# Stick-breaking and forgetting layers: q and k projected with both activation halves in one 512-column matmul

## The chip, the cores and the metric

One core of one Trainium2 chip runs the whole program. The metric is the device time of one execution in microseconds (us); a median of several executions is compared. TensorE (PE) runs the matmuls, its weight loads are a stream of their own (PEld), VectorE (DVE) and ScalarE (ACT) do elementwise work and read the matmul accumulators in PSUM, GpSimd (POOL) does a little elementwise work on SBUF and issues some transfers, SyncE (SP) issues the weight loads.

## The reference

Four transformer layers run in sequence on 256 tokens of width 1024, all in fp32: a differential-attention layer and a MoBA layer (each with memory attention and a squared-ReLU MLP), then a stick-breaking layer and a forgetting layer, each followed by a gated convolution FFN. The change touches the projections of q and k in the last two:

```python
# stick-breaking
a = rmsnorm(h, sb_pre_g[layer])
q, k, v = jnp.split(a @ sb_w_qkv[layer], 3, axis=-1)     # 1024 -> 3 * 1024
o = stick_breaking_attention(split_heads(q), split_heads(k), split_heads(v))   # 16 heads of 64, q scaled by 0.125
...
# forgetting
s_in = rmsnorm(h, kv_norm_g)
kvf = s_in @ w_kvf                                       # k, v and the forget gates
a = rmsnorm(h, fox_pre_g[j])
q = split_heads(a @ fox_w_q[j])
o = forgetting_attention(q, k_sh, v_sh, fcum_sh)
```

## The kernel before

**Precision.** Every fp32 weight and activation of a projection is held as two fp32r tiles, a rounded value and the rest: for weights `whi` and `wlo` (made in `split`, L162 to L190, by one ACT copy and one DVE subtraction from the loaded `raw`), for activations the two halves of `yT`. A product is three matmuls (`mm3`, L211): hi by hi, hi by lo, lo by hi. `yT_tiles` (L247) lays the two activation halves of one 128-row chunk side by side, so that `y[:, k]` is 512 contiguous columns, 256 of the high half and then 256 of the low half.

**q and k of the last two layers.** The layers want q and k with the head dimension on the partitions, so a projection block gives 128 output columns (two heads) by 256 tokens. `layer_sb.qk(pr)` (L825) loads weights for two such blocks of q and two of k (`weights`, L192, in two pieces of four 128-row chunks), and is called for pr = 0, 2, 4, 6; `layer_fox.qk(g)` (L900) does the same for g = 0 to 3 with a gain on the weights, q and k from two matrices. In each, for i in 0 and 1, one accumulator tile of 512 columns takes two blocks, each by `columns_T` (L310): eight chunks of three 256-column matmuls, 24 in all. That makes 16 blocks in each layer, 32 in the program. The accumulators come from `acc_tile` (L83): two buffers of one PSUM bank.

**What reads the accumulators.** In the stick-breaking layer DVE multiplies each half by `R` (the row scales along the tokens, L315) into `qT` and `kT` (L833, L834). In the forgetting layer DVE does it per head, 64 partitions at a time, into `aug` (L915, L916). `quad` and `at` then make scores (`scores`, L354), weights and outputs.

**The up-projections.** `up_pair` (L511) already works in another way: per block eight matmuls of 512 columns with `whi` against both activation halves (L520), then eight of 256 columns with `wlo` against the high half (L522). The result stands in two halves of the bank, which ACT copies (L524) and DVE adds (L525).

**Order.** The text of the kernel is not the order of the engines' queues. A scheduler orders each engine's instructions from the dependences, and only a few places fix an order (`tc.issue_after`). The blocks of qk(4) and qk(6), and of the later g, are interleaved on PE with scores, transposes and outputs of the heads projected before them. Scratch tiles of 512 columns come from `t512`, a ring of five.

Of the kernel before, what the change touches and what calls it, by code (L numbers as in the profile page):

```python
# [10 lines left out]
AF = mybir.ActivationFunctionType  # L11
ALU = mybir.AluOpType
PSUM = bass.MemoryType.PSUM

S, D, P = 256, 1024, 128
NT = S // P
KC = D // P
# [40 lines left out]
def body(ctx, tc, d, out):  # L58
    nc = tc.nc
    mm = nc.tensor.matmul  # L60
    act = nc.scalar.activation
    V = nc.vector
# [11 lines left out]
    def t512(name):  # L74
        return ap_.tile([P, 512], F32, name=name, tag="ev", bufs=E_BUFS)
# [7 lines left out]
    def acc_tile(i=0):  # L83

        tag = ("acc", "pt", "po")[i]
        return pp.tile([P, 512], F32, name="acc", tag=tag, bufs=1 if i else 2)
# [4 lines left out]
    def sc_tile():  # L91
        return pp.tile([P, 512], F32, name="sc", tag="sc", bufs=2)
# [118 lines left out]
    def mm3(acc, a, b, start, stop):  # L211

        mm(acc, lhsT=a[0], rhs=b[0], start=start, stop=False)  # L213
        mm(acc, lhsT=a[0], rhs=b[1], start=False, stop=False)  # L214
        mm(acc, lhsT=a[1], rhs=b[0], start=False, stop=stop)  # L215
# [94 lines left out]
    def columns_T(acc, yT, ws, o):  # L310

        for k in range(KC):
            mm3(acc, tuple(h[:, o:o + P] for h in ws[k]), (yT[0][:, k, :], yT[1][:, k, :]), k == 0, k == KC - 1)
# [194 lines left out]
        V.tensor_tensor(lo, u, hi.bitcast(F32), op=ALU.subtract)  # L508
        return hi, lo

    def up_pair(yT, ws, o, j):  # L511

        s = t512("s")
        for i in range(2):
            b = sc_tile() if j == 0 else pp.tile([P, 512], F32, name="up", tag="ht", bufs=2)
            cs = slice(o + i * P, o + (i + 1) * P)
            for k in range(KC):
                mm(b, lhsT=ws[k][0][:, cs], rhs=yT[2][:, k].rearrange("p a s -> p (a s)"), start=k == 0, stop=False)  # L520
            for k in range(KC):
                mm(b[:, :S], lhsT=ws[k][1][:, cs], rhs=yT[0][:, k], start=False, stop=k == KC - 1)  # L522
            si = s[:, i * S:(i + 1) * S]
            act(si, b[:, S:], AF.Copy)  # L524
            V.tensor_tensor(si, b[:, :S], si, op=ALU.add)  # L525
        return s

    def up_tokens(yT, ws, f):
# [110 lines left out]
    ws = weights(kv_segs("a"), lambda: load_rows(mem, d["mem"], 1))  # L639
# [6 lines left out]
    ws = weights(kv_segs("b"))  # L646
# [173 lines left out]
    def layer_sb(yT, rs, first):  # L820
        w = d["sb_w_qkv_2"][0]
        qT, kT, v = qk_tiles()
        oT = yT_tiles()

        def qk(pr):  # L825

            ws = weights([(w, pr * P, 256, None), (w, D + pr * P, 256, None)])
            for i in range(2):
                acc = acc_tile()
                for j in range(2):  # L830
                    columns_T(acc[:, j * S:(j + 1) * S], yT, ws, (2 * j + i) * P)
                dst = (pr + i) // 4, (pr + i) % 4
                V.scalar_tensor_tensor(qT[dst[0]][:, dst[1]], acc[:, :S], 0.125, R, op0=ALU.mult, op1=ALU.mult)  # L833
                V.tensor_tensor(kT[dst[0]][:, dst[1]], acc[:, S:], R, op=ALU.mult)  # L834

        def vv(c):
            return ([(w, 2 * D + c * 512, 512, None)],
                    lambda t, acc: copy_to(v[:, t, c * 512:(c + 1) * 512], acc, rs[t]))

        def at(pr, t, n=2):  # L840
            quad(qT, kT, lambda b, h: v[:, b, h * 64:(h + 1) * 64], pr, t, True, oT, pr, stick, n)

        projs(yT, [vv(0), vv(1)], after=first)
        R = along_rows(rs)
        qk(0)
        qk(2)
        at(0, 0, 4)
        at(0, 1)
        qk(4)
        at(2, 1)  # L850
        qk(6)
        at(4, 0, 4)
        at(4, 1)
        at(6, 1)
        return OutProj(oT, d["sb_w_o_2"][0], list(range(KC)))


    def layer_fox(yT, rs, first):
        wkv, wq = d["w_kvf_2"], d["fox_w_q_2"][0]
        gk, gq = gain["kv_norm_g_2"], gain["fox_pre_g_2"]  # L860
        v = ap_.tile([P, NT, D], F32, name="vt", tag="vt", bufs=1)
        oT = yT_tiles()
        sums = tc.dram_tile([H2, 3, S], F32, name="sums")
        lf = cst.tile([P, NT, H2], F32, name="lf")
        bf = cst.tile([P, H2], F32, name="bf")
        with tc.issue_after(pows[3].ins):
            nc.gpsimd.dma_start(bf, bc_row(d["b_f_2"], H2))
        with tc.issue_after(last_gelu[0].ins):
            nc.scalar.preload_act_table_set("natural_log_exp_and_others")
        tri = con[:, C_TRI:C_TRI + P]  # L870
        one = con[:, C_ONE:C_ONE + P]
        lu = cst.tile([P, NT, H2], F32, name="lu")

        def v_f(t, acc):

            copy_to(v[:, t, D - 320:], acc[:, :320], rs[t])
            V.scalar_tensor_tensor(lu[:, t], acc[:, 320:], rs[t], bf, op0=ALU.mult, op1=ALU.add)
            if t == 0:
                return
            a = sm.tile([P, NT, H2], F32, name="fa", bufs=1)  # L880
            act(a, lu, AF.Abs)
            act(a, a, AF.Exp, scale=-1.0)
            act(a, a, AF.Ln, bias=1.0)
            V.scalar_tensor_tensor(lf, lu, 0.0, a, op0=ALU.min, op1=ALU.subtract)
            f = tp_tile()
            mm(f[:H2, 0], lhsT=lf[:, 0], rhs=tri, start=True, stop=True)
            mm(f[:H2, 1], lhsT=lf[:, 0], rhs=one, start=True, stop=False)
            mm(f[:H2, 1], lhsT=lf[:, 1], rhs=tri, start=False, stop=True)
            fr = ap_.tile([P, 4, S], F32, name="fr", tag="gb", bufs=1)
            act(fr[:H2, 0], f[:H2, :2], AF.Copy)  # L890
            act(fr[:H2, 2], f[:H2, :2], AF.Copy, scale=-1.0)
            V.memset(fr[:H2, 1], 1.0)
            nc.gpsimd.dma_start(sums, fr[:H2, :3])

        def vv(c0, n):
            return [(wkv, D + c0, n, gk)], lambda t, acc: copy_to(v[:, t, c0:c0 + n], acc, rs[t])

        aug = {}

        def qk(g):  # L900

            for q in (True, False):
                tag = "q" if q else "k"
                aug[g, q] = ap_.tile([P, 4, S], F32, name="aug", tag=tag + str(g % 2), bufs=1)

                row = 0 if q else 1
                nc.gpsimd.dma_start(aug[g, q][64:66], sums[g * 4:(g + 1) * 4, row:row + 2].rearrange("h r s -> r h s"))
            ws = weights([(wkv, g * 256, 256, gk), (wq, g * 256, 256, gq)])
            for i in range(2):
                acc = acc_tile()  # L910
                for j in range(2):
                    columns_T(acc[:, j * S:(j + 1) * S], yT, ws, (2 * j + i) * P)
                for c in range(2):
                    r = slice(c * 64, (c + 1) * 64)
                    V.tensor_tensor(aug[g, False][:64, 2 * i + c], acc[r, :S], R[r], op=ALU.mult)  # L915
                    V.scalar_tensor_tensor(aug[g, True][:64, 2 * i + c], acc[r, S:], 0.125, R[r],  # L916
                                           op0=ALU.mult, op1=ALU.mult)

        def at(g, t):
            nk = (t + 1) * P  # L920
            nb = t + 1
            o = tp_tile("ht")
            n = 2 if t else 4
            for h0 in range(0, 4, n):
                sv, = scores([[aug[g, True][:66, h0 + c] for c in range(n)]],
                             [[aug[g, False][:66, h0 + c] for c in range(n)]], t, nk)
                pT = weights_T(soft(sv, True, nk), nk)
                for j in range(0, n, 2):
                    for b in range(nb):
                        for c in range(2):  # L930
                            h = 4 * g + h0 + j + c
                            mm(o[c * 64:(c + 1) * 64, (h0 + j) // 2], lhsT=v[:, b, h * 64:(h + 1) * 64],
                               rhs=pT[:, (j + c) * nb + b], start=b == 0, stop=b == nb - 1)
            out_T(oT, t, o[:, :2], 2 * g)

        projs(yT, [([(wkv, 2 * D - 320, 320 + H2, gk)], v_f)])
        R = along_rows(rs)
        projs(yT, [vv(0, 384)])
        qk(0)
        qk(1)  # L940
        at(0, 0)
        at(0, 1)
        projs(yT, [vv(384, 320)])
        at(1, 0)
        qk(2)
        at(2, 0)
        at(1, 1)
        qk(3)
        at(3, 0)
        at(2, 1)  # L950
        at(3, 1)
        return OutProj(oT, d["fox_w_o_2"][0], list(range(KC)))
# [95 lines left out]
```

## Time and profile before

| | us |
|---|---|
| median of 3 runs | 1245.14 (1244.16 to 1249.25) |
| the profiled execution | 1245.2 |
| its span, first to last instruction | 1243.4 |
| PE busy in the span | 1222.5 |
| DVE busy | 905.6 |
| ACT busy | 753.9 |
| POOL busy | 44.8 |

The profiled execution is 0.06 us from the median; 1.8 us of it lie outside the span. PE's busy time counts overlapping matmuls once, and a matmul's recorded duration is longer than the distance to the start of the next one, so a pace is read from start to start. The granted TensorE clock is 0.998 of full speed over the span. The stick-breaking layer's q and k blocks run from 644.4 to about 705 us and the forgetting layer's from about 953 to 1016 us.

### The profile page before, as it was taken

To read this page: it belongs to the slowest core of one execution; us is meant where nothing else is said; L and a number is where in the kernel's file an instruction comes from. 1 tells how busy PE (TensorE), PEld (TensorE's weight loads), DVE (VectorE), ACT (ScalarE), POOL (GpSimd) and SP (SyncE) were. 2 spreads that over 40 slices of the span, in tenths; PEclk is the share of its full clock that TensorE was granted. 3 is DMA by queue.
4 is the path that set the end of the run, shared out by engine and by line. 5 is a ranking of instruction groups with operands and counts; after the bars stand their busy time and mean duration, and the time that the engine had idled before them with its cause. 6 is when DMAs were issued, how large, how long until landed. Compare 5 with 4: busy or idle time off the path is not lost.

```text
span 1243.4 us, 17840 instructions
## 1 busy us (share of the span) xinstructions
PE 1222.5 (98%) x6703; PEld 1022.0 (82%) x6703; DVE 905.6 (73%) x1677; ACT 753.9 (61%) x1363; POOL 44.8 (4%) x77
## 2 busy tenths in 40 slices
PE   8999999999999999999999999999999999999997
PEld 6876788888877788888889878888889997888886
DVE  5768756565776765756667888877788876987775
ACT  7665654454666654545555778666677755866663
POOL 1200100000000000000000010000001001000000
PEclk9999999999999999999999999999999999999999
DMA  9734356465452365655474416655537453565550
GB/s 322 220 135 140 123 179 220 152 207 200 154 185 102 103 203 179 215 181 183 156 232 158 135 58 206 207 181 197 203 111 244 143 158 115 193 205 180 179 193 34
DMA packets 125957, 214.21 MB, mean 172 GB/s; under 512 B 5280, under 2 KB 78304, under 8 KB 125872
## 3 DMA queue, kind: packets, MB, share of 16 engines
q1 hardware_dynamic: 123392, 207.25, 49.3%
q0 software_dynamic: 2336, 5.77, 1.7%
q8 instruction: 52, 0.85, 0.3%
q14 instruction: 33, 0.27, 0.1%
q10 hardware_dynamic: 144, 0.07, 0.0%
HBM read 211.96 MB, written 1.10 MB: 171 GB/s over the span
## 4 chain that ended last, share of the span: by engine, by line
PE 88%; DVE 4%; ACT 4%; issue 2%; DMA 1%; POOL 1%; SPq 0%; POOLq 0%; DVEq 0%; ACTq 0%
PE acc L213 12%; PE acc L215 12%; PE acc L214 12%; PE up L520 10%; PE sc L520 10%; PE up L522 5%; PE sc L522 5%; PE acc L292 4%; PE acc L293 4%; PE acc L295 4%; PE sc L360 2%; PE tp L399 2%; PE tp L449 2%; DVE wlo L175 2%; PE tp L257 1%
## 5 line engine op out<-in xcount | busy, mean ns | idle before, releaser
L175 DVE TENSOR_TENSOR wlo<-raw,whi 128x1024 fp32r<-128x1024 f32 x336 | 405.8, 1220 | 108.9 <-ACT whi L174 85.9
L174 ACT ACTIVATE whi<-raw 128x1024 fp32r<-128x1024 f32 x336 | 346.0, 1055 | 104.5 <-PE acc L215 60.2
L213 PE MATMUL acc<-whi,u 128*128 128x512 f32 x432 | 169.2, 392 | 0.0
L214 PE MATMUL acc<-wlo,u 128*128 128x512 f32 x432 | 168.6, 390 | 0.0
L215 PE MATMUL acc<-whi,u 128*128 128x512 f32 x432 | 168.0, 390 | 0.0
L520 PE MATMUL sc<-yT,whi 128*128 128x512 f32 x544 | 136.6, 391 | 0.0
L520 PE MATMUL up<-yT,whi 128*128 128x512 f32 x544 | 135.9, 392 | 0.0
L292 PE MATMUL acc<-whi,yT 128*128 128x512 f32 (+3 forms) x336 | 131.5, 394 | 0.0
L293 PE MATMUL acc<-wlo,yT 128*128 128x512 f32 (+3 forms) x336 | 130.0, 390 | 0.0
L520 PEld LDWEIGHTS sc<-yT,whi 128*128 128x128 f32 x544 | 99.7, 188 | 19.0
L520 PEld LDWEIGHTS up<-yT,whi 128*128 128x128 f32 x544 | 98.6, 189 | 18.1
L607 DVE SCALAR_TENSOR_TENSOR cv<-s,conv,cv 128x254 f32<-128x254 f32 (+1 forms) x160 | 76.1, 479 | 36.1 <-ACT cv L605 34.9
L215 PEld LDWEIGHTS acc<-whi,u 128*128 128x128 f32 x432 | 81.0, 188 | 17.9 <-DVE u L508 0.4
L213 PEld LDWEIGHTS acc<-whi,u 128*128 128x128 f32 x432 | 81.3, 188 | 16.3 <-ACT u L507 0.9
L214 PEld LDWEIGHTS acc<-wlo,u 128*128 128x128 f32 x432 | 81.3, 188 | 15.1
L295 PE MATMUL acc<-whi,yT 128*128 128x512 f32 (+3 forms) x336 | 84.5, 385 | 0.0
L185 DVE SCALAR_TENSOR_TENSOR wlo<-raw,g_late,whi 128x256 fp32r<-128x256 f32 (+4 forms) x128 | 68.2, 580 | 17.5 <-ACT whi L184 17.3
L522 PEld LDWEIGHTS up<-yT,wlo 128*128 128x128 f32 x544 | 74.2, 190 | 5.3
L522 PEld LDWEIGHTS sc<-yT,wlo 128*128 128x128 f32 x544 | 74.2, 190 | 5.2
L184 ACT ACTIVATE whi<-raw,g_late 128x256 fp32r<-128x256 f32 (+4 forms) x128 | 64.7, 577 | 20.4 <-PE acc L214 11.1
L522 PE MATMUL up<-yT,wlo 128*128 128x256 f32 x544 | 75.9, 282 | 0.0
L522 PE MATMUL sc<-yT,wlo 128*128 128x256 f32 x544 | 75.8, 282 | 0.0
(199 smaller groups left out, 1931.8 us busy)
## 6 DMA issues: line engine op xcount, KB each, us to landing
raw<-in_w_up SPq DMA_DIRECT2D x88, 512.0 KB, 4.5
raw<-in_w_down SPq DMA_DIRECT2D x22, 1024.0 KB, 5.0
raw<-in_a_w_up SPq DMA_DIRECT2D x16, 1024.0 KB, 5.3
raw<-in_a_w_down SPq DMA_DIRECT2D x16, 1024.0 KB, 5.0
raw<-in_b_w_up SPq DMA_DIRECT2D x16, 1024.0 KB, 5.3
raw<-in_b_w_down SPq DMA_DIRECT2D x16, 1024.0 KB, 5.0
raw<-in_sb_w_qkv SPq DMA_DIRECT2D x16, 512.0 KB, 5.0
raw<-in_a_w_in SPq DMA_DIRECT2D x6, 1024.0 KB, 7.5
```

The lines of the kernel that those rows point to most:

```text
L174: act(hv, rv[:, k0:k1], AF.Copy)
L175: V.tensor_tensor(lv, rv[:, k0:k1], hv.bitcast(F32), op=ALU.subtract)
L185: V.scalar_tensor_tensor(lv[:, k - k0, o:e], rv[:, k, o:e], gk, hv[:, k - k0, o:e].bitcast(F32), op0=ALU.mult, op1=ALU.subtract)
L213: mm(acc, lhsT=a[0], rhs=b[0], start=start, stop=False)
L214: mm(acc, lhsT=a[0], rhs=b[1], start=False, stop=False)
L215: mm(acc, lhsT=a[1], rhs=b[0], start=False, stop=stop)
L292: mm(acc, lhsT=h, rhs=ws[k][0], start=k == 0, stop=False)
L293: mm(acc, lhsT=h, rhs=ws[k][1], start=False, stop=False)
L295: mm(acc, lhsT=tslice(yT, k, t)[1], rhs=ws[k][0], start=False, stop=k == KC - 1)
L520: mm(b, lhsT=ws[k][0][:, cs], rhs=yT[2][:, k].rearrange("p a s -> p (a s)"), start=k == 0, stop=False)
L522: mm(b[:, :S], lhsT=ws[k][1][:, cs], rhs=yT[0][:, k], start=False, stop=k == KC - 1)
L607: V.scalar_tensor_tensor(hi[:, sh:], pi[:, :S - sh], cw(tap, ch), hi[:, sh:], op0=ALU.mult, op1=ALU.add)
```

## The change

`both_T` takes the matmul loops out of `up_pair`, and `added` the copy and the sum, with a scale. The q and k projections call these for each block, on an accumulator tile of its own, into a scratch tile `z` of 256 columns. In the stick-breaking layer GpSimd then multiplies `z` by `R` into `qT` or `kT`; in the forgetting layer DVE multiplies the two heads' 64 rows of `z` by `R` into `aug`. `up_pair` itself computes what it did.

```diff
+    def both_T(b, yT, ws, o):
+        cs = slice(o, o + P)
+        for k in range(KC):
+            mm(b, lhsT=ws[k][0][:, cs], rhs=yT[2][:, k].rearrange("p a s -> p (a s)"), start=k == 0, stop=False)
+        for k in range(KC):
+            mm(b[:, :S], lhsT=ws[k][1][:, cs], rhs=yT[0][:, k], start=False, stop=k == KC - 1)
+
+    def added(b, dst, scale=1.0):
+        act(dst, b[:, S:], AF.Copy, scale=scale)
+        V.scalar_tensor_tensor(dst, b[:, :S], scale, dst, op0=ALU.mult, op1=ALU.add)
...
     def up_pair(yT, ws, o, j):
...
-            si = s[:, i * S:(i + 1) * S]
-            act(si, b[:, S:], AF.Copy)
-            V.tensor_tensor(si, b[:, :S], si, op=ALU.add)
+            both_T(b, yT, ws, o + i * P)
+            added(b, s[:, i * S:(i + 1) * S])
...
             for i in range(2):          # layer_sb.qk
-                acc = acc_tile()
-                for j in range(2):
-                    columns_T(acc[:, j * S:(j + 1) * S], yT, ws, (2 * j + i) * P)
                 dst = (pr + i) // 4, (pr + i) % 4
-                V.scalar_tensor_tensor(qT[dst[0]][:, dst[1]], acc[:, :S], 0.125, R, op0=ALU.mult, op1=ALU.mult)
-                V.tensor_tensor(kT[dst[0]][:, dst[1]], acc[:, S:], R, op=ALU.mult)
+                for j, to in enumerate((qT, kT)):
+                    acc, z = acc_tile(), t512("cq")[:, :S]
+                    both_T(acc, yT, ws, (2 * j + i) * P)
+                    added(acc, z, 1.0 if j else 0.125)
+                    nc.gpsimd.tensor_tensor(to[dst[0]][:, dst[1]], z, R, op=ALU.mult)
...
             for i in range(2):          # layer_fox.qk
-                acc = acc_tile()
                 for j in range(2):
-                    columns_T(acc[:, j * S:(j + 1) * S], yT, ws, (2 * j + i) * P)
-                for c in range(2):
-                    r = slice(c * 64, (c + 1) * 64)
-                    V.tensor_tensor(aug[g, False][:64, 2 * i + c], acc[r, :S], R[r], op=ALU.mult)
-                    V.scalar_tensor_tensor(aug[g, True][:64, 2 * i + c], acc[r, S:], 0.125, R[r],
-                                           op0=ALU.mult, op1=ALU.mult)
+                    acc, z = acc_tile(), t512("cq")[:, :S]
+                    both_T(acc, yT, ws, (2 * j + i) * P)
+                    added(acc, z)
+                    for c in range(2):
+                        r = slice(c * 64, (c + 1) * 64)
+                        V.scalar_tensor_tensor(aug[g, j == 1][:64, 2 * i + c], z[r], 0.125 if j else 1.0, R[r],
+                                               op0=ALU.mult, op1=ALU.mult)
```

## Rows read from the trace of the kernel before

**Rows 1.** The page, busy us, share of the span and instructions of each engine:
```profile
PE 1222.5 (98%) x6703; PEld 1022.0 (82%) x6703; DVE 905.6 (73%) x1677; ACT 753.9 (61%) x1363; POOL 44.8 (4%) x77
```

**Rows 2.** The page, chain of work that ended last, share of the span by engine:
```profile
PE 88%; DVE 4%; ACT 4%; issue 2%; DMA 1%; POOL 1%; SPq 0%; POOLq 0%; DVEq 0%; ACTq 0%
```

**Rows 3.** Windows over both layers' q and k stretches:
```profile
core 0: us, PE busy (x) PEld busy (x) DVE busy (x) ACT busy (x) POOL busy (x), PEclk, DMA share, GB/s
644.00:668.00 24.00, 24.00 (x203) 23.74 (x203) 13.29 (x17) 10.16 (x12) 0.00 (x0) 1.00 0.73 244
668.00:692.00 24.00, 23.83 (x189) 20.26 (x186) 23.44 (x40) 18.05 (x30) 0.00 (x0) 1.00 0.35 118
692.00:716.00 24.00, 23.95 (x168) 19.46 (x166) 19.22 (x35) 16.34 (x26) 0.00 (x0) 1.00 0.45 146
...
953.00:987.00 34.00, 34.00 (x275) 32.52 (x274) 25.76 (x90) 20.86 (x58) 1.10 (x2) 1.00 0.57 186
987.00:1020.00 33.00, 32.91 (x263) 30.31 (x262) 25.93 (x74) 20.11 (x48) 1.66 (x3) 1.00 0.45 147
```

**Rows 4.** Timeline of PE, start us and duration, in qk(0), 75 matmuls apart:
```profile
644.88 0.28 PE L213 MATMUL acc<-yT,whi 128*128 128x256 f32 x1
...
653.88 0.28 PE L213 MATMUL acc<-yT,whi 128*128 128x256 f32 x1
```

**Rows 5.** Timeline of PE in the up-projection; the window cuts the last row:
```profile
773.20 1.98 PE L520 MATMUL sc<-yT,whi 128*128 128x512 f32 x8
775.02 1.11 PE L522 MATMUL sc<-yT,wlo 128*128 128x256 f32 x8
775.97 2.00 PE L520 MATMUL sc<-yT,whi 128*128 128x512 f32 x8
...
778.76 1.55 PE L520 MATMUL up<-yT,whi 128*128 128x512 f32 x6
```

**Rows 6.** Groups by line and form: busy us, mean ns, idle before and its releaser:
```profile
L213 PE MATMUL acc<-yT,whi 128*128 128x256 f32 x256 | 74.5, 291 | 0.0
...
L525 DVE TENSOR_TENSOR s<-sc,s 128x256 f32<-128x256 f32 x68 | 28.6, 421 | 38.6 <-ACT s L524 38.1
...
L524 ACT ACTIVATE s<-sc 128x256 f32<-128x256 f32 x68 | 26.0, 382 | 77.1 <-PE sc L522 76.8
...
L915 DVE TENSOR_TENSOR aug<-acc,R 64x256 f32<-64x256 f32 x16 | 6.7, 420 | 2.2 <-PE acc L215 2.0
L916 DVE SCALAR_TENSOR_TENSOR aug<-acc,R 64x256 f32<-64x256 f32 x16 | 6.6, 413 | 0.0
```

**Rows 7.** The same groups of DVE alone, 644 to 716 us:
```profile
L175 DVE TENSOR_TENSOR wlo<-raw,whi 128x1024 fp32r<-128x1024 f32 x20 | 24.0, 1219 | 10.2 <-ACT whi L174 9.9 <-PE tp L399 0.2
...
L436 DVE TENSOR_TENSOR ka<-ka,kb 128x512 f32<-128x512 f32 x7 | 4.8, 687 | 0.1
L833 DVE SCALAR_TENSOR_TENSOR qT<-acc,R 128x256 f32<-128x256 f32 x8 | 3.3, 416 | 2.1 <-PE acc L215 2.1
L834 DVE TENSOR_TENSOR kT<-acc,R 128x256 f32<-128x256 f32 x8 | 3.3, 411 | 0.0
```

**Rows 8.** Timeline of POOL, start us and duration, with idle before and releaser:
```profile
85.49 1.04 POOL L222 TENSOR_TENSOR rstd<-ms,mhalf 128x4 f32<-128x4 f32 x1 [46.96 <-DVE ms L229]
...
630.25 0.56 POOL L222 TENSOR_TENSOR rstd<-ms,mhalf 128x1 f32<-128x1 f32 x1 [1.96 <-DVE ms L240]
723.32 0.58 POOL L108 DMA_DIRECT2D gr<-in_ffn_pre_g  x1 [92.51 <-DVE ka L436]
```

**Rows 9.** Waits of PEld, 644 to 740 us: total, times, longest:
```profile
PEld sc L360 <- DVE kT L834: 0.9, 3, 0.4
```

**Rows 10.** Waits of PEld, 953 to 1040 us:
```profile
PEld sc L360 <- DVE aug L916: 0.5, 2, 0.2
```

**Rows 11.** Timeline of ACT, the weight splits of qk(4):
```profile
665.48 3.91 ACT L174 ACTIVATE whi<-raw 128x1024 fp32r<-128x1024 f32 x4 [7.62 <-PE acc L214]
```

**Rows 12.** Line L213, durations ns min/median/max:
```profile
L213 PE MATMUL acc<-yT,whi x256: 277/283/471, 644.4 to 1015.9; 128*128 128x256 f32 x128
```

More of the change, by code (lines that the diff above doesn't have):

```diff
@@ L517, in up_pair @@
             b = sc_tile() if j == 0 else pp.tile([P, 512], F32, name="up", tag="ht", bufs=2)
[L518 to L522, printed above, removed]
-            si = s[:, i * S:(i + 1) * S]
-            act(si, b[:, S:], AF.Copy)
-            V.tensor_tensor(si, b[:, :S], si, op=ALU.add)
+            both_T(b, yT, ws, o + i * P)
+            added(b, s[:, i * S:(i + 1) * S])
         return s
```

## Prediction

> **What bounds the kernel.** I read the page's busy times first, then its chain, then windows over the two stretches that change, and last the start-to-start pace of the matmuls. PE is busy for 98% of the span [rows 1] and carries 88% of the chain that ended last [rows 2]. In the windows the reader is to see that PE leaves almost nothing over in either stretch: 71.78 of 72 us from 644 to 716, 66.91 of 67 us from 953 to 1020, at full granted clock [rows 3]. The second thing to see is which engine stands next: DVE, with 23.44 of 24 us from 668 to 692, where attention runs between the projections, but only 13.29 of 24 before that [rows 3]. So a saving counts if it shortens PE's own stream, and a cost counts if it makes PE wait; work on ACT, DVE or POOL is free as long as it is not late for PE.
>
> **The matmuls.** A block of 128 output columns goes from 24 matmuls of 256 columns to eight of 512 and eight of 256. The columns streamed are the same, 6144. What differs is the number of matmuls. Before: 75 matmuls in 9.00 us from start to start, 0.120 us each, so 24 x 0.120 = 2.88 us a block [rows 4]. After: the up-projection is the new form exactly, and its blocks start at 773.20, 775.97 and 778.76, so 2.78 us a block in the mean [rows 5]. The difference is 0.10 us, and over 32 blocks 3.2 us. It is small because the long matmul costs nearly as much as two short ones: from 773.20 to 775.02 the eight long ones take 0.2275 us each, against 2 x 0.120 = 0.240 us [rows 4, 5]; what is fixed in a matmul is thus about 0.0125 us, and eight fewer of them are the 0.10 us. The bounds: nothing, if scores and transposes break up the new stream as often as the old, and 5.2 us, if also the excess over the typical matmul goes. That excess is read on L213: its mean is 291 ns and its median 283 ns, times 256 that is 2.0 us [rows 6, 12]. I take 3.2 us.
>
> The Trainium skill (TensorE: Matmul & The Clock Gate, "Wait — 56ns, not 53.3ns?") gives the fixed part of a warm matmul as about 2.5 ns, which would make the change worth 32 x 8 x 2.5 ns, some 0.6 us by estimate. The trace does not agree: its rows give 12.5 ns, five times that.
>
> **Order inside a block.** Before, the first three matmuls need `whi` and `wlo` of the first chunk; after, all `wlo` are needed only behind eight long matmuls, 1.8 us into the block. This can only help at a start. I count nothing for it, since no listed wait of these blocks is as long as that.
>
> **Evacuation.** Before, DVE reads the accumulator once per block in the stick-breaking layer (0.416 us for q, 0.411 us for k [rows 7]) and twice, by heads, in the forgetting layer (0.420 and 0.413 us [rows 6]). After, ACT copies a half (0.382 us) and DVE adds the other (0.421 us), as in the up-projection [rows 6]; then POOL (first layer) or two DVE operations (second) multiply by R.
> - ACT gains 32 x 0.382 = 12.2 us, half in each stretch. It is busy for 44.6 of 72 us and 41.0 of 67 us there [rows 3], so 6.1 us more is hidden by its idle time; without that cover it would cost those 6.1 us in each.
> - DVE in the stick-breaking layer exchanges one operation of 0.41 us for one of 0.42 us: nothing.
> - DVE in the forgetting layer gains one operation a block, 16 x 0.42 = 6.7 us, on 51.7 of 67 us [rows 3]. The 15.3 us idle hide it; without cover it would be all 6.7 us.
> - POOL gains 16 multiplies of 128x256. The trace has none. From below: the DVE multiply of this shape, 0.411 us [rows 7]. From above: POOL's power operation, whose duration rises from 0.56 us at one column to 1.04 us at four, 0.16 us a column [rows 8], which would make some 41 us. The nearest row in what is computed is DVE's, in the engine POOL's fixed part. I take 0.56 us plus 256 columns at DVE's pace between its 256 and 512 column forms, (687 - 411) / 256 = 1.1 ns [rows 7], together 0.84 us, and keep 41 us as the far bound. At 0.84 us a multiply takes a third of a block's 2.78 us and delays nobody on POOL.
>
> POOL's queue holds nothing else there: after the power operation at 630.25 its next entry is the transfer of `gr` at 723.32, which waits 92.51 us for a buffer that this very attention frees [rows 8]. The multiplies must stand ahead of it, or the attention would never end; the last of them falls near 707, so the transfer keeps its place. No other queue is moved: the weight loads on SP are the same.
>
> **Late arrivals at the scores.** The scores wait for the evacuated q and k. Before, the last block's chain is two DVE operations, 0.83 us. After, it is copy, add and multiply: 0.38 + 0.42 + 0.84 = 1.64 us in the first layer, and 0.38 + 0.42 + 2 x 0.42 = 1.64 us in the second. That is 0.8 us later. The waits that show it now are five, 0.9 us in three on `kT` and 0.5 us in two on `aug` [rows 9, 10]. If each grew by 0.8 us it would cost 4.0 us, if other blocks fill in, nothing. Blocks of later heads are at hand in most places; I take 0.3 of it, 1.2 us.
>
> **Sum.** On the profiled execution: 1245.2 - 3.2 + 1.2 = 1243.2 us, which is 1241.4 us of span and 1.8 us around it. The median of the runs is 1245.14, so nothing needs to be shifted. About 0.5% (6.2 us) is what a measurement can tell from no change, and this gain of 0.16% is below it.
>
> **Rivals.**
> - *PE waits for accumulators (slower).* There are two, and each now holds one block, not two, so a block must be evacuated within the 2.78 us of the next. Copy and add take 0.80 us, which leaves 1.98 us for both queues. One weight split ahead on each queue, 3.91 / 4 = 0.98 us on ACT and 1.22 us on DVE [rows 11, 7], is 2.20 us: a stall of 0.22 us at least; four splits in a row as at 665.48 would be 3.91 + 0.80 - 2.78 = 1.9 us. It decides from 0.3 us a block on: 32 x 0.3 = 9.6 us, less 3.2, and the time is 1251.6 us. For it: DVE's 23.44 of 24 us. Against it: from 668 to 705 PE spends 37 us on eight blocks with attention between, 4.6 us each, and before 668 both queues are half idle [rows 3]. Chance 0.16.
> - *POOL and DVE get in each other's way (no change).* If every multiply after 668, about ten, takes DVE's time as well, that is 8.4 us against the 5.3 us that DVE has idle from 668 to 716 [rows 3]: 3.1 us late, and 1246.3 us. No row here shows the two at work together. Chance 0.17. The Trainium skill (SBUF — State Buffer, "SBUF: two separate sides") has such a rule: an operation of DVE with two SBUF inputs and one of GpSimd that reads SBUF hold a shared port pair in turn, and one blocks the other for its whole length. The split and the sums of the stick-breaking weights have two SBUF inputs, so the rule would apply here; no row yet bears on it.
> - *The saving does not come (no change).* The interleaving eats the 3.2 us and the late arrivals remain: 1246.4 us. For it: the scheduler makes a new order from new durations. Against it: most of the blocks before 668 run without a break. Chance 0.05.
> - *Everything helps (faster).* 3.2 us, the 2.0 us of excess and the 1.4 us of waits on `kT` and `aug` all go: 6.6 us, 1238.6 us. Chance 0.09.
> - *The POOL multiply costs what the power operation suggests (slower).* From 2.78 us on POOL sets the pace; at 41 us, 16 of them are 656 us, largely exposed: some 1850 us. Chance 0.03, since a power is much more work per element than a product.
>
> **How the numbers follow.** The forecast has 0.50 and is 1243.2 us. Faster by over 0.5% (below 1238.9) is the fourth rival alone, 0.09; slower by over 0.5% (above 1251.4) the first and the fifth, 0.19; the rest, 0.72, is no change. The range goes from 1238.0, just beyond the case where all helps, to 1252.0, just beyond the first rival's point; the fifth rival and the longer stalls of the first lie outside it.
>
> **What would show it.** In the changed profile: 256 matmuls of 512 columns and 256 of 256 columns in place of 768, with a block's start-to-start at 2.78 us where nothing is between; PE's busy share in both stretches as before; the scores' waits longer by under 1 us. The first rival would show as waits of PE for ACT or DVE at the first matmul of a block; the second as split or `ka`, `kb` operations of DVE longer than 1.22 and 0.69 us while POOL works; the fifth as POOL busy in the stretch from 644 to 716. The prediction is wrong if the order on PE changes so that some stage runs out of work: a few us at the end of either layer would be enough, in either direction.

## The result and the profile after

The changed kernel takes 1254.57 us in the median of 8 runs (1247.98 to 1256.1), the kernel before 1245.34 us in 8 runs of its own beside it. The ratio is 1.0063 with an interval of 1.0052 to 1.0075: slower by 0.63%, and outside the predicted range. The eight runs fall into two groups. Six have a granted clock of 0.994 or 0.995 and take 1253.9 to 1256.1 us; two have 0.999 and take 1248.0 and 1248.2 us. So about 6.9 us go with the lower clock (medians of the groups 1255.0 and 1248.1 us), and some 2.7 us are lost without it.

The profiled execution took 1254.85 us. The page of the changed kernel, busy time by engine, beside [rows 1]:

```profile
PE 1226.4 (98%) x6447; PEld 1010.6 (81%) x6447; DVE 914.8 (73%) x1693; ACT 763.6 (61%) x1395; POOL 62.2 (5%) x93
```

Shares do not show the loss: PE is still 98% busy. ACT has gained 9.7 us, DVE 9.2 and POOL 17.4, and PE has the 256 matmuls fewer that the change makes. To find the place, I compare the same four events in both kernels, the `rstd` operation of POOL after each part. First the changed kernel, timeline of POOL:

```profile
631.59 0.56 POOL L222 TENSOR_TENSOR rstd<-ms,mhalf 128x1 f32<-128x1 f32 x1 [1.95 <-DVE ms L240]
...
757.76 0.56 POOL L222 TENSOR_TENSOR rstd<-ms,mhalf 128x1 f32<-128x1 f32 x1 [1.93 <-DVE ms L240]
...
946.97 0.55 POOL L222 TENSOR_TENSOR rstd<-ms,mhalf 128x1 f32<-128x1 f32 x1 [4.23 <-DVE ms L240]
...
1064.95 0.56 POOL L222 TENSOR_TENSOR rstd<-ms,mhalf 128x1 f32<-128x1 f32 x1 [1.92 <-DVE ms L240]
```

The kernel before, the same view (its first event is in [rows 8], at 630.25):

```profile
747.27 0.56 POOL L222 TENSOR_TENSOR rstd<-ms,mhalf 128x1 f32<-128x1 f32 x1 [1.93 <-DVE ms L240]
...
936.10 0.55 POOL L222 TENSOR_TENSOR rstd<-ms,mhalf 128x1 f32<-128x1 f32 x1 [4.22 <-DVE ms L240]
...
1055.31 0.56 POOL L222 TENSOR_TENSOR rstd<-ms,mhalf 128x1 f32<-128x1 f32 x1 [1.92 <-DVE ms L240]
```

The lag is 1.3 us before the stick-breaking layer, 10.5 us behind it, 10.9 us before the forgetting layer and 9.6 us behind it. So the stick-breaking layer loses 9.2 us, and the forgetting layer gains 1.2. Of the 1.3 us, 1.0 is there at the second `rstd` operation, at 14.15 us against 13.15, before anything that was changed; the up-projections of the earlier layers, whose sum on DVE now has a scale, add under 0.1 us.

Inside the losing layer, windows of the changed kernel (columns as in [rows 3]):

```profile
669.00:693.00 24.00, 22.39 (x104) 16.00 (x102) 18.44 (x32) 14.35 (x27) 4.90 (x4) 0.79 0.27 88
...
672.00:675.00 3.00, 2.82 (x12) 2.24 (x13) 2.29 (x3) 1.51 (x3) 0.13 (x1) 0.75 0.81 329
675.00:678.00 3.00, 3.00 (x10) 1.90 (x8) 2.64 (x7) 0.78 (x3) 0.00 (x0) 0.50 0.72 224
678.00:681.00 3.00, 3.00 (x7) 1.78 (x7) 1.82 (x5) 2.94 (x6) 1.10 (x1) 0.50 0.33 131
681.00:684.00 3.00, 3.00 (x12) 2.52 (x11) 3.00 (x8) 0.91 (x2) 0.00 (x0) 0.54 0.00 0
...
645.00:735.00 90.00, 85.61 (x474) 65.94 (x473) 66.05 (x101) 57.32 (x94) 16.82 (x16) 0.94 0.42 136
...
735.00:760.00 25.00, 22.90 (x129) 17.41 (x128) 20.43 (x37) 15.15 (x33) 3.94 (x7) 1.00 0.38 126
```

The same stretches of the kernel before, which reaches the end of the second one 10.5 us earlier:

```profile
645.00:735.00 90.00, 89.78 (x662) 76.29 (x661) 71.28 (x118) 58.24 (x92) 1.68 (x3) 1.00 0.42 137
735.00:749.50 14.50, 13.16 (x63) 10.23 (x62) 11.69 (x20) 8.28 (x19) 2.24 (x4) 1.00 0.51 181
```

Two things are to be seen. The granted clock falls to 0.50, TensorE's 1.2 GHz in place of 2.4: the shares of the first and the last of the four slices put this at about 673.5 to 683.8 us. The missing shares of the four slices are 0.75 + 1.5 + 1.5 + 1.4 = 5.1 us of PE's work. And PE is idle for 4.4 + 2.1 = 6.5 us over the two stretches, against 0.2 + 1.3 = 1.6 before: 4.9 us more. Less the saving in matmuls, 16 blocks by 0.09 (below), 1.4 us, this is 8.6 of the 9.2 us. The last 0.6 us I could not place, and the 5.1 us are less than the 6.9 us between the two groups of runs. Of the 4.9 us, 2.6 are waits of PE for `kT` (2.8 us against 0.2) and 2.5 are two later waits for ACT (`ka`, 1.6, and `pT`, 0.9) that PE does not have before; a shorter wait for `y` takes 0.2 off.

What PE does there, timeline of PE in the changed kernel:

```profile
645.77 2.07 PE L516 MATMUL acc<-yT,whi 128*128 128x512 f32 x8
647.68 1.11 PE L518 MATMUL acc<-yT,wlo 128*128 128x256 f32 x8
648.63 2.00 PE L516 MATMUL acc<-yT,whi 128*128 128x512 f32 x8
...
651.42 2.00 PE L516 MATMUL acc<-yT,whi 128*128 128x512 f32 x8
...
654.22 2.00 PE L516 MATMUL acc<-yT,whi 128*128 128x512 f32 x8
...
668.27 0.94 PE L360 MATMUL sc<-kT,qT 64*128 64x128 f32 x12
669.14 1.43 PE L516 MATMUL acc<-yT,whi 128*128 128x512 f32 x5
672.18 0.49 PE L360 MATMUL sc<-kT,qT 64*128 64x128 f32 x4 [1.61 <-POOL kT L840]
...
674.07 2.07 PE L360 MATMUL sc<-kT,qT 64*128 64x256 f32 x4
...
715.91 0.49 PE L360 MATMUL sc<-kT,qT 64*128 64x128 f32 x4 [1.17 <-POOL kT L840]
...
717.45 1.13 PE L360 MATMUL sc<-kT,qT 64*128 64x256 f32 x4
```

And in the kernel before, the same place, PE and then DVE:

```profile
667.64 0.94 PE L360 MATMUL sc<-kT,qT 64*128 64x128 f32 x12
668.51 0.39 PE L213 MATMUL acc<-yT,whi 128*128 128x256 f32 x1
...
669.65 0.49 PE L360 MATMUL sc<-kT,qT 64*128 64x128 f32 x4 [0.17 <-DVE kT L834]
...
666.57 2.36 DVE L175 TENSOR_TENSOR wlo<-raw,whi 128x1024 fp32r<-128x1024 f32 x2 [3.82 <-ACT whi L174]
668.84 0.42 DVE L833 SCALAR_TENSOR_TENSOR qT<-acc,R 128x256 f32<-128x256 f32 x1
669.18 0.41 DVE L834 TENSOR_TENSOR kT<-acc,R 128x256 f32<-128x256 f32 x1
```

The blocks are as forecast, 2.79 and 2.80 us from start to start, after a first one of 2.86. But when the projections of qk(2) end, PE makes twelve score matmuls, some matmuls of the next block, and then the scores of the last head pair, which need the last `kT`. PE's order puts little projection between the two: six matmuls of 256 columns before, 1.0 us, and five of 512 after, 1.4 us. Before, the waiting scores could start 2.0 us after the first ones and PE waited 0.17 us; now they start 3.9 us after, and PE stands for 1.61 us. The clock falls behind that stand, from about 1.3 us after its end: the score group at 674.07 takes 2.07 us, the like group at 717.45 takes 1.13. A second stand of 1.17 us is at 715.91, after qk(6), and no clock fall follows it.

Why the last `kT` is late is read from the queues of ACT, DVE and POOL ahead of it, timeline of the changed kernel, one engine after the other:

```profile
666.11 2.95 ACT L174 ACTIVATE whi<-raw 128x1024 fp32r<-128x1024 f32 x3
668.97 0.36 ACT L522 ACTIVATE cq<-acc 128x256 f32<-128x256 f32 x1
...
659.16 2.90 DVE L175 TENSOR_TENSOR wlo<-raw,whi 128x1024 fp32r<-128x1024 f32 x2
...
667.72 2.36 DVE L175 TENSOR_TENSOR wlo<-raw,whi 128x1024 fp32r<-128x1024 f32 x2 [1.23 <-PE acc L518]
670.00 0.42 DVE L523 SCALAR_TENSOR_TENSOR cq<-acc,cq 128x256 f32<-128x256 f32 x1
670.33 1.22 DVE L175 TENSOR_TENSOR wlo<-raw,whi 128x1024 fp32r<-128x1024 f32 x1
...
659.32 1.65 POOL L840 TENSOR_TENSOR kT<-cq,R 128x256 f32<-128x256 f32 x1 [3.24 <-DVE cq L523]
663.78 0.74 POOL L840 TENSOR_TENSOR kT<-cq,R 128x256 f32<-128x256 f32 x1 [0.57 <-DVE cq L523]
...
670.50 1.63 POOL L840 TENSOR_TENSOR kT<-cq,R 128x256 f32<-128x256 f32 x1 [3.18 <-DVE cq L523]
```

The block is done at about 668.3. ACT's copy stands behind three weight splits and starts at 668.97, DVE's sum behind two and starts at 670.00. POOL's product starts at 670.50 and takes 1.63 us, not the 0.74 us of a product that runs alone (663.78): a split of DVE has begun at 670.33 and runs to 671.55, and the product ends 0.6 us after it. The other direction is there too: the DVE pair at 659.16, beside a product, takes 2.90 us, the pair at 667.72 takes 2.36. Queueing behind splits is not new: in the kernel before, the block is done at about 667.7 and DVE's two operations start only at 668.84, 1.1 us later, behind a pair of splits. From the block's end to the last `kT` it is 1.9 us before and 3.8 us after. Over the layer, the products for k (minimum, median and maximum, ns) and PE's wait for them (total, times, longest):

```profile
L840 POOL TENSOR_TENSOR kT<-cq,R x8: 736/1376/1657, 652.5 to 714.2; 128x256 f32<-128x256 f32 x8
...
PE sc L360 <- POOL kT L840: 2.8, 2, 1.6
```

Theory: the product of the last `kT` on POOL, lengthened by DVE, makes PE stand with too little other work before it, and the clock falls behind the stand. Rivals: that PE is short of accumulators (the first rival of the prediction), that the new matmul order itself disturbs the layer, and that the length of the chain does it wherever the product runs.

### The profile page after: what moved, and what is told of

It is laid out like the page before. It is cut to its first block, busy times and chain, and to the rows that moved or that the text cites. A ratio compares the mean times of both kernels' runs of the same rounds, so it can differ in the third digit from the quotient of the medians.

```text
span 1253.1 us, 17383 instructions
## 1 busy us (share of the span) xinstructions
PE 1226.4 (98%) x6447; PEld 1010.6 (81%) x6447; DVE 914.8 (73%) x1693; ACT 763.6 (61%) x1395; POOL 62.2 (5%) x93
## 4 chain that ended last, share of the span: by engine, by line
PE 87%; DVE 4%; ACT 3%; issue 2%; DMA 1%; POOL 1%; SPq 0%; POOLq 0%; DVEq 0%; ACTq 0%
PE up L516 10%; PE sc L516 10%; PE acc L215 10%; PE acc L213 10%; PE acc L214 10%; PE up L518 5%; PE sc L518 5%; PE acc L516 5%; PE acc L292 4%; PE acc L293 4%; PE acc L295 4%; PE sc L360 3%; PE acc L518 2%; PE tp L399 2%; DVE wlo L175 1%
## 5 line engine op out<-in xcount | busy, mean ns | idle before, releaser
L213 PE MATMUL acc<-whi,u 128*128 128x512 f32 x432 | 169.1, 391 | 0.0
L213 PEld LDWEIGHTS acc<-whi,u 128*128 128x128 f32 x432 | 81.3, 188 | 16.4 <-ACT u L507 0.9
L292 PEld LDWEIGHTS acc<-whi,yT 128*128 128x128 f32 x336 | 64.2, 191 | 11.2 <-issue 0.8
```

The lines of the kernel that those rows point to most:

```text
L292: mm(acc, lhsT=h, rhs=ws[k][0], start=k == 0, stop=False)
```

## The experiments

Times are medians; the kernel before took 1244.6 to 1244.9 us on the same chips; each ratio is to that.

**Which layer.** One kernel has the change in the forgetting layer alone, one in the stick-breaking layer alone.

```diff
                 dst = (pr + i) // 4, (pr + i) % 4
-                for j, to in enumerate((qT, kT)):
-                    acc, z = acc_tile(), t512("cq")[:, :S]
-                    both_T(acc, yT, ws, (2 * j + i) * P)
-                    added(acc, z, 1.0 if j else 0.125)
-                    nc.gpsimd.tensor_tensor(to[dst[0]][:, dst[1]], z, R, op=ALU.mult)
+                acc = acc_tile()
+                for j in range(2):
+                    columns_T(acc[:, j * S:(j + 1) * S], yT, ws, (2 * j + i) * P)
+                V.scalar_tensor_tensor(qT[dst[0]][:, dst[1]], acc[:, :S], 0.125, R, op0=ALU.mult, op1=ALU.mult)
+                V.tensor_tensor(kT[dst[0]][:, dst[1]], acc[:, S:], R, op=ALU.mult)
```

This is the first of the two against the changed kernel; the second puts the old lines back in `layer_fox.qk` in the same way.

> Only the forgetting layer projects in the new way; the stick-breaking layer is as before. Theory (all the loss is made in the stick-breaking layer, where scores wait for the late GpSimd product and TensorE's clock then falls): the forgetting layer by itself gains the 1.2 us that the two traces show there between 10.85 and 9.65 us of lag, so about 1244.1 us, clock 0.998 to 0.999. Rival (the accumulators that hold one block instead of two cost something in both layers): 1247 us or more.

> Only the stick-breaking layer projects in the new way. Theory: the whole loss, 1254.6 + 1.2 = 1255.8 us in most runs, clock 0.994 to 0.995, and a few runs near 1249 us with clock 0.999. Rival (accumulators, in both layers): about half of the loss, 1250 us.

Forgetting alone: 1243.8 us, 0.9991 (0.9983 to 1.0000). Stick-breaking alone: 1256.52 us, 1.0092 (1.0078 to 1.0106), with clocks of 0.992 to 0.994. None of the four runs of the second is near 1249 us. The two effects, -1.1 and +11.6 us, leave all the loss in the stick-breaking layer; the forgetting layer gains about what the lag showed, at the edge of what the interval resolves. The +11.6 is not all made by the change: in its profiled execution (1258.72 us) the clock is at 0.50 for some 7 us near 90 us too, where nothing is changed, and 3.1 us are lost there; between the `rstd` events the stick-breaking layer itself takes 9.3 us more, as in the changed kernel.

**The product on DVE.** The same change, but DVE multiplies by `R`.

```diff
-                    nc.gpsimd.tensor_tensor(to[dst[0]][:, dst[1]], z, R, op=ALU.mult)
+                    V.tensor_tensor(to[dst[0]][:, dst[1]], z, R, op=ALU.mult)
```

> The changed kernel with the product by R in the stick-breaking layer on VectorE instead of GpSimd; accumulators and matmuls as in the changed kernel. Theory (the late and stretched GpSimd product): no score waits for more than half a microsecond, the clock stays at 0.998 or above in all runs, and the saving on the matmuls comes through: 1243 us, between 1241 and 1246. Rival (accumulators): unchanged, 1252 us or more. Rival (VectorE is the bound from 668 to 692 us and gets 16 more operations of 0.42 us): 1249 us, clock 0.998.

It took 1245.38 us, 1.0003 (0.9995 to 1.0012), and the clock is 0.999 in every run. Its timeline of PE at the place, and its windows:

```profile
666.65 0.94 PE L360 MATMUL sc<-kT,qT 64*128 64x128 f32 x12
667.52 2.11 PE L516 MATMUL acc<-yT,whi 128*128 128x512 f32 x8
669.47 0.63 PE L518 MATMUL acc<-yT,wlo 128*128 128x256 f32 x4
670.32 0.49 PE L360 MATMUL sc<-kT,qT 64*128 64x128 f32 x4 [0.22 <-DVE kT L840]
...
668.00:692.00 24.00, 23.78 (x136) 18.00 (x135) 22.56 (x43) 17.80 (x33) 0.00 (x0) 1.00 0.26 88
...
716.00:735.00 19.00, 17.05 (x102) 11.59 (x102) 16.23 (x30) 14.36 (x29) 1.98 (x3) 1.00 0.09 29
```

With the product on DVE the wait is 0.22 us and the clock stays at 1.00. Most of that is order, not an earlier `kT`. The waiting scores start 3.67 us after the first ones, hardly sooner than the 3.91 us with the product on POOL, since on DVE a split stands between the sum and the product (668.38, 668.71 and 669.85 us). But the scheduler has put twelve matmuls of the next block (eight long, four short, 2.58 us) ahead of the waiting scores, not five (1.43 us). So of the 1.39 us by which the stand is shorter, 1.15 are order and 0.24 an earlier `kT`. No run kept the order and changed the engine alone, and why the scheduler orders the two kernels differently is not shown. Matmuls, copy and sum in their new form are not the cause; the loss of some 0.6% hangs on the engine of the product and the order that comes with it. It is no gain over before either, though, and the last window shows where a part goes: PE stands idle for 1.95 of 19 us at the end of the attention, where the kernel before has none.

**Only one of the two products.** k on DVE and q on POOL, and the reverse.

```diff
-                    nc.gpsimd.tensor_tensor(to[dst[0]][:, dst[1]], z, R, op=ALU.mult)
+                    (V if j else nc.gpsimd).tensor_tensor(to[dst[0]][:, dst[1]], z, R, op=ALU.mult)
...
+                    (nc.gpsimd if j else V).tensor_tensor(to[dst[0]][:, dst[1]], z, R, op=ALU.mult)
```

> The changed kernel with the product by R on VectorE for k, which is the last of each pair, and on GpSimd for q. Theory (only the product that comes last before the scores is on the path): as with both on VectorE, 1244 to 1246 us, clock 0.998 or above. Rival (any GpSimd product in this stretch costs, since it and VectorE stop each other): half of the loss, 1249 to 1250 us.

> The mirror of it: the product by R on VectorE for q and on GpSimd for k. Theory: the last product is still on GpSimd, so the wait and in most runs the fall of the clock remain, 1251 to 1256 us, clock below 0.997. Rival (any GpSimd product costs): 1249 to 1250 us, as with the other half.

With k on DVE: 1243.94 us, 0.9997 (0.9988 to 1.0007). With q on DVE and k on POOL: 1251.7 us, 1.0040 (1.0024 to 1.0056); one of its seven executions took 6865.67 us at full clock and is not in the ratio. Of the other six, four have a clock of 0.994 or 0.995 and take 1251.4 to 1252.5 us, two have 0.999 and take 1246.1 and 1246.5 us: the clock is again worth some 5.6 us. PE's wait in the first, and the window with the wait in the second:

```profile
PE sc L360 <- DVE kT L840: 0.5, 2, 0.3
```

```profile
668.00:692.00 24.00, 22.33 (x110) 15.85 (x106) 18.70 (x34) 13.70 (x26) 2.59 (x2) 0.79 0.27 88
```

So half of the products, those of k, carry most of the loss. POOL as such is no obstacle: eight products of q on it cost nothing measurable. Here too the order goes with the engine of k: the waiting scores start 3.76 us after the first ones in the first kernel and 3.91 us in the second, with twelve matmuls ahead of them in the first and five in the second.

**Work in the gap.** Nine matmuls of 512 columns into an accumulator that nobody reads are put behind the last matmul of qk(2), ahead of the scores. They are extra work, about 2.0 us of PE.

```diff
+            last_mm[:] = [mm(b[:, :S], lhsT=ws[k][1][:, cs], rhs=yT[0][:, k], start=False, stop=k == KC - 1)]
...
+        def between():
+            with tc.issue_after(last_mm[0].ins):
+                idle = acc_tile(2)
+                for _ in range(9):
+                    mm(idle, lhsT=yT[0][:, 0, :P], rhs=yT[2][:, 0].rearrange("p a s -> p (a s)"), start=True, stop=True)
...
+        between()
```

> The changed kernel with nine extra matmuls of 512 columns, about 2.0 us, into an accumulator that nobody reads, queued behind the last block of qk(2) and ahead of the first scores: TensorE works where it waited 1.6 us for the product on GpSimd. Theory (that wait lets the clock fall, and the fall costs some 6.5 us): the clock is 0.998 or above in all runs and the time about 1248 us, although 2.0 us of work are added. Rival (the fall of the clock has another cause): most runs stay at clock 0.995 and 1254 us or more.

It took 1249.11 us, 1.0034 (1.0022 to 1.0046): faster than the changed kernel, though it does more. The first stand is down from 1.61 to 0.90 us, not to nothing, because the five matmuls of the next block no longer stand ahead of the waiting scores. The window over it shows no fall:

```profile
PE sc L360 <- POOL kT L840: 2.1, 2, 1.2
...
668.00:692.00 24.00, 22.03 (x138) 16.98 (x137) 21.74 (x37) 17.67 (x34) 4.17 (x4) 1.00 0.25 88
```

In this profile the late product still costs its wait, without the fall. The theory wanted 0.998 or above in all runs, and that did not come: three of the six have 0.996 and take 1250.1 to 1250.8 us, three have 0.998 or 0.999 and take 1247.6 to 1248.1 us, so the runs that were not profiled may hold a shorter fall somewhere. A clock of 0.996 need not come from this place: 1 of the 22 runs of the kernel before beside it has it too, at 1248.3 us.

**A third accumulator.** In the stick-breaking layer alone, the blocks go round three accumulators, not two. (The expectation speaks of both layers; the edit is in this one, where the loss is.)

```diff
-                    acc, z = acc_tile(), t512("cq")[:, :S]
+                    acc, z = acc_tile((0, 0, 2)[n_q[0] % 3]), t512("cq")[:, :S]
+                    n_q[0] += 1
```

> The changed kernel with three accumulators for the q and k blocks in both layers (two of the old ring and the bank that the output projection takes later). Theory (late GpSimd product): the wait of the scores for kT and the fall of the clock stay, 1252 to 1256 us. Rival (accumulators): 1246 us or less.

It took 1251.7 us, 1.0055 (1.0043 to 1.0067), with clocks of 0.993 to 0.996. The wait has not moved:

```profile
PE sc L360 <- POOL kT L841: 2.8, 2, 1.6
```

So accumulators are not what PE waits for. The time is a little under what the theory gave.

**The old matmuls with the new product.** The kernel before with its 24 matmuls and its accumulator of two blocks; DVE copies each half out with the scale, and POOL multiplies by `R`. There is no copy on ACT and no sum.

```diff
                 dst = (pr + i) // 4, (pr + i) % 4
-                V.scalar_tensor_tensor(qT[dst[0]][:, dst[1]], acc[:, :S], 0.125, R, op0=ALU.mult, op1=ALU.mult)
-                V.tensor_tensor(kT[dst[0]][:, dst[1]], acc[:, S:], R, op=ALU.mult)
+                for j, to in enumerate((qT, kT)):
+                    z = t512("cq")[:, :S]
+                    V.tensor_scalar(z, acc[:, j * S:(j + 1) * S], 1.0 if j else 0.125, None, op0=ALU.mult)
+                    nc.gpsimd.tensor_tensor(to[dst[0]][:, dst[1]], z, R, op=ALU.mult)
```

> The kernel before, with its 24 matmuls a block, where VectorE copies the accumulator halves of the stick-breaking layer with their scale and GpSimd multiplies by R: the product on GpSimd alone, without the new matmuls. Theory (the late product on GpSimd is the loss, whatever the matmuls): the scores wait for kT by 1.5 us or more and the clock falls to 0.994 to 0.996 in most runs, 1251 to 1258 us. Rival (the loss needs the new matmul form or the new accumulators): 1247 us or less, clock 0.998 or above.

It took 1255.19 us, 1.0080 (1.0060 to 1.0100), with clocks from 0.990 to 0.997. PE waits for POOL as in the changed kernel, and longer:

```profile
PE sc L360 <- POOL kT L836: 3.6, 2, 1.9
```

The copy on DVE and the product on POOL make the whole loss in the median, without a single changed matmul. But the profiled execution is the fastest of the six (1249.71 us), and its windows speak against a simple rule for the clock:

```profile
668.00:692.00 24.00, 22.05 (x170) 18.59 (x169) 22.74 (x38) 16.03 (x26) 7.46 (x6) 1.00 0.34 115
692.00:716.00 24.00, 21.77 (x148) 17.58 (x148) 16.58 (x23) 14.00 (x21) 4.55 (x4) 0.93 0.42 134
```

The longest wait for `kT` in all the profiles, 1.95 us up to 670.32, has no fall behind it. The second, 1.64 us up to 710.24, has a fall of about 3.4 us in place of ten.

**Is there a gain behind the wait?** Two kernels try to collect the 2.7 us of the matmuls in full. In the first, POOL does nothing in the stick-breaking layer: the sum goes straight into `qT`, the queries' row scale is applied where the mask is added, and DVE multiplies k by `R`. The second is k on DVE with a third accumulator.

```diff
-        V.tensor_tensor(a, sv, m, op=ALU.add)
+        V.scalar_tensor_tensor(a, sv, r, m, op0=ALU.mult, op1=ALU.add)
...
+                    z = t512("cq")[:, :S] if j else to[dst[0]][:, dst[1]]
...
+                    if j:
+                        V.tensor_tensor(to[dst[0]][:, dst[1]], z, R, op=ALU.mult)
```

> A version to beat both: the changed kernel without GpSimd in the stick-breaking layer; the sum for q goes straight into qT and the row scale of the queries is applied where the scores get their mask, in one operation that is there already; k is multiplied by R on VectorE. VectorE has 8 operations of 0.42 us fewer than with both products on it. Theory: 1243 us, between 1241 and 1245, clock 0.998 or above. Rival (the order at the end of the layer decides, not the number of operations): 1245 to 1247 us.

> A version to beat both: the product by R on VectorE for k and on GpSimd for q, and a third accumulator for the stick-breaking blocks. Theory: the accumulators cost a little by themselves, since the third one took about 3 us off the changed kernel: 1241.5 us, between 1240 and 1243. Rival (what the third accumulator took off was a matter of the order around the wait, which is gone here): 1243 to 1245 us.

They took 1245.45 us, 1.0009 (1.0001 to 1.0018), and 1244.87 us, 1.0005 (0.9996 to 1.0014). In both the rival holds: the gain does not arrive. Over 645 to 735 us PE is idle for 2.2 us in the first of the two kernels and 2.5 us in the second, as it is for 2.5 us with both products on DVE; with k alone on DVE it is 0.9 us, and in the kernel before 0.2. From the `rstd` event before the stick-breaking layer to the one behind it, the kernel before takes 117.0 us, the two kernels 117.8 and 117.2, both products on DVE 118.5 and k alone on DVE 117.2: none keeps the 1.4 us that the matmuls save in this layer. They come back, in part or whole, as idle time of PE, which waits for what DVE and ACT do for the attention. That is read from the traces; no run tested it. No version here is measurably faster than the kernel before.

## Why the prediction was wrong

- **The bound** was right: PE's stream sets the time. So was the warning that a cost counts if it makes PE wait.
- **The matmuls** came as forecast. The block takes 2.79 and 2.80 us where 2.78 was written, so 32 blocks save about 2.7 us, not 3.2; the forgetting layer shows its share as 1.2 us of lag made up, and the layer alone as 0.9991.
- **Evacuation.** ACT and DVE are hidden by the cover that was named. The product on POOL was forecast at 0.84 us, between bounds of 0.411 and 41. It takes 0.74 us alone, 1.04 to 1.66 us where an operation of DVE runs beside it, 1.05 in the mean of the 16. Alone the estimate was good, in the mean a fifth low; where it counted, the last `kT`, it was half of what was needed.
- **Late arrivals at the scores is the step that failed.** It had the scores' last operand 0.8 us later, and hid seven tenths of that under blocks of later heads, 1.2 us in all. Measured from the first scores to the waiting ones, it came 1.9 us later (3.9 against 2.0), and PE's waits on `kT` grew by 2.6 us in this layer alone (2.8 against 0.2). The 0.8 us were right for the durations, 1.5 us of undisturbed operations against 0.75. What was left out is the product's growth beside a split, 0.9 us, and the queues: 0.7 us behind splits on ACT and 0.7 on DVE, 0.3 us more than the one stand of 1.1 us behind splits before. The cover was wrong as well: PE's order, fixed before the run, has 1.4 us of projection there against 1.0 before, so it hid 0.5 of the 1.9 us and not seven tenths, and the kernel before was already short by 0.17 us. Where DVE makes the product, `kT` comes nearly as late and the order has 2.6 us there. Waits on `kT` were known, 0.9 us in three of PE's weight loads [rows 9]; a wait that is there already has no slack, and a later arrival shows in it in full.
- **The clock was a missing term.** The forecast kept the full granted clock of [rows 3]. In most runs that is the larger part of the 9.2 us, 6.9 us by the two groups of runs and 5.1 by the windows of the profile: the runs without the fall take 1248.1 us, which is still above 1243.2 but inside the predicted range.
- **Rivals.** PE short of accumulators: refuted, since a third one leaves the wait as it was. POOL and DVE in each other's way: the mechanism is the one at work, but its place was wrong. The sum was made on DVE's busy time, and gave 1246.3 us; DVE was not even full there (18.44 of 24 us). What it does is lengthen one product on the path. The sign that was named for it is there too: a pair of splits takes 2.90 us in place of 2.36. The saving that does not come: it came, and in the versions without a late product it was spent again at the end of the attention. POOL as dear as a power: no.
- **What would make it wrong** was named, an order on PE by which a stage runs out of work, a few us, but it was given no price. It happened inside the layer, not at its end, and was the smaller part: the larger is what followed on the clock.

## What to carry to other kernels

Where a value goes through a chain of engines to a waiting matmul, count what stands ahead of it in each queue and not the durations alone; look up how much work the waiting engine's order has ahead of the wait, since a new order can change that more than the chain (five matmuls or twelve here); and look up whether the trace of before already shows a wait there: if so, no slack is left. Where PE is full at full clock, price a new stand of PE also with what the clock may do behind it, since in most runs here that cost more than the stand itself. If an elementwise step has to move to GpSimd, move the operand that is not awaited: the products of q cost nothing measurable there, those of k 5 to 8 us (ratios 1.0040 against 0.9997; medians 1251.7 against 1243.94).

## What the runs showed of the hardware

- **POOL beside DVE.** The 128x256 product of POOL takes 0.74 us alone and 1.63 us where a split of DVE, 1.22 us long, has begun 0.17 us before it; it ends 0.6 us behind the split. A pair of splits takes 2.90 us in place of 2.36 when a product starts 0.16 us after it. In the changed kernel's profile eight of the 16 products take 1.04 to 1.66 us, and all eight end 0.6 us behind an operation of DVE that began just before them; the other eight take 0.74 or 0.75 us. The Trainium skill (SBUF — State Buffer, "SBUF: two separate sides") says that a DVE operation with two SBUF inputs and a GpSimd operation that reads SBUF exclude each other for their whole length. These rows agree with it: the split has two SBUF inputs, and the product's end is the split's end plus most of a product.
- **The clock.** PE, busy without a break from 645.8 us on, stood for 1.61 us at 670.6; behind it the granted clock was at 1.2 GHz for about 10 us and then back at 2.4. The profiles with the change in the stick-breaking layer alone, with q on DVE and with a third accumulator have the same stand of 1.61 us and a fall of the same length. Stands of 0.90 to 1.22 us in this layer, in these profiles and in the one with work in the gap, show no fall behind them. In the profile of the old matmuls with the new product a stand of 1.95 us shows none and one of 1.64 us a fall of about 3.4 us. Six of eight runs of the changed kernel, and four of six with k on POOL and q on DVE, have the lower mean clock that goes with a fall; the others have the same program and do not. So a fall follows such a stand in most runs but not in all, and what decides stays open.
